# VectorE's paired instructions in the chunk scan of layer 2, joined into one each

## The chip, the core and the metric

The kernel runs on one core of one Trainium2 chip. The metric is device time in microseconds (us) of one launch; less is better. The engines of the core are named as the profile names them: PE (TensorE matmuls), DVE (VectorE), ACT (ScalarE), POOL (GpSimd) and SP (SyncE, which issues nearly all DMAs here).

## What is computed

Two blocks of a language model on one sequence of 1024 tokens with 1024 channels, in float32: layer 1 (a recurrent branch beside latent attention), layer 2 (a state-space layer), then a block with a short convolution, stick-breaking attention and an MLP. The change lies in layer 2, whose scan over chunks of 128 tokens is this, cut to what matters:

```python
xf = x * dt                                   # per head of 64 channels, 32 heads, 4 groups of 8 heads
cs = cumsum(dt * a_neg) within a chunk        # 8 chunks of 128 tokens
cb = einsum('bclgn,bcsgn->bcgls', cc, bc)     # per group, 128 x 128 per chunk
y_diag = einsum('bcghls,bcsghp->bclghp', cb * exp(cs_l - cs_s) (causal), xf)
states = einsum('bclgn,bclghp->bcghpn', bc, xf * exp(cs_end - cs))
prev   = the states carried over the chunks   # h * exp(cs_end) + state
y_off  = einsum('bclgn,bcghpn->bclghp', cc, prev) * exp(cs)
y = (y_diag + y_off + d_skip * x) * silu(z)
```

## The kernel before

Each float32 matmul is made as three products of rounded halves (`mm3`, lines 189, 193 and 194: high by high, low by high, high by low). A cast on ACT makes the high half and a subtraction in `lo` (line 260) the low one, on DVE in the scan and on POOL elsewhere. Weights come through `weights` in sets of three tiles `wr`, `wh`, `wl`: a DMA, a cast on ACT (line 180), a subtraction.

`phase_b` is layer 2. Its work comes in 8 units u (half a group, 4 heads, 256 channels), and each unit in 4 steps of two chunks, so 32 steps. A step has two parts:

- `stage1`: four transposes on PE into PSUM (line 891); `Xf`, the transposed x times dt and times w2, a [128 x 512] half each (line 898), then its halves `Xh` (ACT, line 902) and `Xl` (DVE, 260). `L`, [128 x 2 chunks x 4 heads x 128], is loaded from `csd` by one DMA (line 907), goes through eight Relus (911) and one Exp (913) on ACT, is multiplied by the group's `cbm` on DVE (916), and split into `Lh` (ACT, 918) and `Ll` (DVE). The tile `L` has one buffer, so the next load waits for this `Ll`. Then the states of both chunks (matmuls into a `t` bank, lines 934 to 940 for `hs`, `hh`, `hl`).
- `stage2`: the matmuls of y_off into a bank of PSUM, `et` loaded with exp(cs) by four DMAs (line 966), `zt` loaded from DRAM; then on DVE: `et` times that bank (971, or 973 and 974 in a unit's first step, whose first chunk has no state before it), the skip term (976, one instruction per tile of 128 channels), the sum with y_diag (988, four per step, 64 partitions each), and the product with z (991, one per tile). The result goes to DRAM (992); ACT squares it (997) and DVE adds the squares up (999 or 1002).

In `et` the 512 columns stand as (chunk, tile, token), in `zt` as (tile, chunk, token).

Between the steps stand projections: 48 matmuls of 512 columns each into one `g` tile (two banks), whose results go through ACT (lines 810, 812 or 873), and DVE. They are independent of the scan until their own unit needs them, and the loop at the end of `phase_b` deals them out by `PATTERN`; once all are made, `part` puts matmuls of the layer's output projection in their place. At the end of a group `prep_bc` makes the next group's `cbm` and the halves of B and C (lines 846 to 860).

The Python order is not the order on the chip: a scheduler places each engine's instructions when the program is built, by its own estimate of their durations, and each engine then works strictly in that order. PSUM has two `g` tiles, two `t` banks and one bank each of `u` and `w` here; the matmuls of y_off and y_diag take `u` and `w` in turn, so one of them can only start when DVE has read the bank before.

Of the kernel before, what the change touches and what calls it, by code (L numbers as in the profile page):

```python
# [12 lines left out]
A = mybir.AluOpType  # L13
# [5 lines left out]
HN = 512  # L19
# [30 lines left out]
class K:  # L50
# [38 lines left out]
    def v(self, name, i=0, n=1):  # L89
        o, _ = VEC[name]  # L90
        return self.vec[:, o + i:o + i + n]
# [657 lines left out]
    def phase_b(self):  # L749
# [14 lines left out]
        ps = first.pop(0)  # L764
# [115 lines left out]
        def stage1(u, cpair):  # L880

            g, hg = divmod(u, 2)
            h0 = 8 * g + 4 * hg
            c0 = 2 * cpair
            th, tl, ch, cl, cbm = bc[g]
            xt = xs[u]

            ps = self.t1()
            for c in range(2):
                for p in range(2):  # L890
                    nc.tensor.transpose(ps[:, c * 256 + p * 128:c * 256 + p * 128 + 128],
                                        xt[p][:, (c0 + c) * 128:(c0 + c) * 128 + 128], self.ident)
            Xf = P("Xf")
            for j, f in enumerate((dt_t, w2_t)):
                for c in range(2):
                    fb = f[:, (c0 + c) * 32 + h0:(c0 + c) * 32 + h0 + 4]
                    q = slice(c * 256, c * 256 + 256)
                    nc.vector.tensor_tensor(Xf[:, j * HN + c * 256:j * HN + c * 256 + 256].rearrange("p (h d) -> p h d", h=4),
                                            ps[:, q].rearrange("p (h d) -> p h d", h=4),
                                            fb[:, :, None].to_broadcast([128, 4, 64]), op=A.mult)  # L900
            Xh, Xl = R("Xh"), R("Xl")
            nc.scalar.copy(Xh, Xf)
            self.lo(nc.vector, Xl, Xf, Xh)

            L = self.tag("L", "L")
            Lv = L.rearrange("p (c h l) -> p c h l", c=2, h=4)
            nc.sync.dma_start(L.rearrange("p (c x) -> p c x", c=2),
                              csd[c0:c0 + 2, h0:h0 + 4, :].rearrange("c h l -> c (h l)").partition_broadcast(128))
            for c in range(2):
                for h in range(4):  # L910
                    nc.scalar.activation(Lv[:, c, h, :], Lv[:, c, h, :], AF.Relu, scale=-1.0,  # L911
                                         bias=cs_t[:, (c0 + c) * 32 + h0 + h:(c0 + c) * 32 + h0 + h + 1])
            nc.scalar.activation(L, L, AF.Exp, scale=-1.0)
            cv = cbm.rearrange("p (c l) -> p c l", c=8)
            for c in range(2):
                nc.vector.tensor_tensor(Lv[:, c], Lv[:, c], cv[:, c0 + c:c0 + c + 1, :].to_broadcast([128, 4, 128]), op=A.mult)
            Lh, Ll = R("Lh"), R("Ll")
            nc.scalar.copy(Lh, L)
            self.lo(nc.vector, Ll, L, Lh)

            prev = []
            pst = self.t1()
            for c in range(2):
                s = slice((c0 + c) * 128, (c0 + c) * 128 + 128)
                q = slice(HN + c * 256, HN + c * 256 + 256)
                prev.append(hst[u][1] if c0 + c else None)
                if c0 + c == 7:
                    break
                self.mm3(pst[:, c * 256:c * 256 + 256], (th[:, s], tl[:, s]), (Xh[:, q], Xl[:, q]), True, True)
                hn = self.ph.tile([128, 256], F32, tag="hs", bufs=2, name=self.nm("hs"))  # L930
                q = pst[:, c * 256:c * 256 + 256]
                if c0 + c:
                    dv = dec[:, h0:h0 + 4, c0 + c][:, :, None].to_broadcast([128, 4, 64])
                    nc.vector.tensor_tensor(hn.rearrange("p (h d) -> p h d", h=4), hst[u][0].rearrange("p (h d) -> p h d", h=4), dv, op=A.mult)
                    nc.vector.tensor_tensor(hn, hn, q, op=A.add)
                else:
                    nc.vector.tensor_copy(hn, q)
                hh = self.ph.tile([128, 256], F32R, tag="hh", bufs=4, name=self.nm("hh"))
                hl = self.ph.tile([128, 256], F32R, tag="hl", bufs=4, name=self.nm("hl"))
                nc.scalar.copy(hh, hn)  # L940
                self.lo(nc.vector, hl, hn, hh)
                hst[u] = hn, (hh, hl)
            stg[u, cpair] = Xh, Xl, Lh, Ll, prev

        def stage2(u, cpair):
            g, hg = divmod(u, 2)
            h0 = 8 * g + 4 * hg
            c0 = 2 * cpair
            th, tl, ch, cl, cbm = bc[g]
            xt = xs[u]  # L950
            Xh, Xl, Lh, Ll, prev = stg.pop((u, cpair))
            cols = slice(c0 * 128, c0 * 128 + 256)

            poff = self.u1()
            for c in range(2):
                if prev[c]:
                    hh, hl = prev[c]
                    s = slice((c0 + c) * 128, (c0 + c) * 128 + 128)
                    for p in range(2):
                        q = slice(p * 128, p * 128 + 128)  # L960
                        self.mm3(poff[:, c * 256 + p * 128:c * 256 + p * 128 + 128], (hh[:, q], hl[:, q]), (ch[:, s], cl[:, s]), True, True)
            et = self.E("et")
            ev = et.rearrange("p (c q l) -> p c q l", c=2, q=2)
            for j in range(2):
                for p in range(2):
                    nc.sync.dma_start(ev[64 * j:64 * j + 64, :, p, :], ecd[c0:c0 + 2, h0 + 2 * p + j, :].partition_broadcast(64))
            zt = self.E("zt")
            zv = zt.rearrange("p (q x) -> p q x", q=2)
            nc.sync.dma_start(zv, self.zd[u * 256:u * 256 + 256, cols].rearrange("(q p) x -> p q x", q=2))
            if c0:  # L970
                nc.vector.tensor_tensor(et, et, poff, op=A.mult)
            else:
                nc.vector.memset(et[:, 0:256], 0.0)
                nc.vector.tensor_tensor(et[:, 256:], et[:, 256:], poff[:, 256:], op=A.mult)
            for p in range(2):
                nc.vector.scalar_tensor_tensor(ev[:, :, p, :], xt[p][:, cols].rearrange("p (c l) -> p c l", c=2), v("d_skip", 4 * g + 2 * hg + p),
                                               ev[:, :, p, :], op0=A.mult, op1=A.add)

            for c in range(2):
                pd = self.u1()  # L980
                for p in range(2):
                    q = slice(c * 256 + p * 128, c * 256 + p * 128 + 128)
                    s = slice(c * HN + p * 256, c * HN + p * 256 + 256)
                    self.mm3(pd[:, p * 256:p * 256 + 256], (Xh[:, q], Xl[:, q]), (Lh[:, s], Ll[:, s]), True, True)
                pv = pd.rearrange("p (q j l) -> p q j l", q=2, j=2)
                for j in range(2):
                    r = slice(64 * j, 64 * j + 64)
                    nc.vector.tensor_tensor(ev[r, c], ev[r, c], pv[r, :, j, :], op=A.add)
            for p in range(2):
                z = zv[:, p, :].rearrange("p (c l) -> p c l", c=2)  # L990
                nc.vector.scalar_tensor_tensor(z, ev[:, :, p, :], 0.5, z, op0=A.mult, op1=A.mult)
            nc.sync.dma_start(self.yd[u * 256:u * 256 + 256, cols].rearrange("(q p) x -> p q x", q=2), zv)

            if g not in acc2:
                acc2[g] = P("acc2")
            sq = et
            nc.scalar.activation(sq, zt, AF.Square)
            if hg == 0:
                nc.vector.tensor_tensor(acc2[g][:, cols], sq[:, 0:256], sq[:, 256:], op=A.add)
            else:  # L1000
                for p in range(2):
                    nc.vector.tensor_tensor(acc2[g][:, cols], acc2[g][:, cols], sq[:, p * 256:p * 256 + 256], op=A.add)
                if cpair % 2:
                    n = cpair // 2
                    s = slice(n * HN, n * HN + HN)
                    ps = self.u1()
                    nc.tensor.matmul(ps, self.ones, acc2[g][:, s], start=True, stop=True)
                    self.rstd_from(acc2[g][:, s], ps, 1.0 / 512, 1e-6)
                    nc.sync.dma_start(self.rsd[g:g + 1, s], acc2[g][0:1, s])
# [919 lines left out]
```

## Time and profile before

| what | value |
|---|---|
| runs, us | 2761.08, 2748.82, 2758.09; median 2758.09 |
| profiled execution, us | 2749.49 |
| its span, first to last instruction, us | 2747.7 |
| busy in the span, us | PE 2590.2, DVE 1933.3, ACT 1438.8, POOL 655.1 |
| mean granted TensorE clock | 0.975 of full |
| the scan of layer 2 in the trace | from about 570 to 1280 us |
| attention of the second block in the trace | from about 1680 to 1990 us |

A busy share is an average over stages with different limits; idle time of an engine that nobody waits for costs nothing. A wait is put down to the instruction whose end released it.

### The profile page before, as it was taken

Reading aid. Unit: us, or ns where it says so; the run is one execution under the profiler, and the core shown is the slowest. Engines: PE = TensorE matmul, PEld = TensorE weight load, DVE = VectorE, ACT = ScalarE, POOL = GpSimd, SP = SyncE. Lnnn points to the kernel's source line nnn. Section 1 sums busy time; section 2 is a strip of 40 time slices with the busy share of each in tenths; the row PEclk is TensorE's granted clock in tenths of the full one; section 3 lists DMA queues with packets and bytes.
Section 4 is the critical chain, followed back from the end, with each engine's and each line's share of the span. In section 5 each row is a group of like instructions: output and inputs, shape, how many; then the busy total and the mean of one; then the engine's idle time right before and its main releaser. Section 6 shows DMA issues by size and latency. Waiting matters only on the chain. (4 is left out here: it accounts for less than half of the span.)

```text
span 2747.7 us, 34501 instructions
## 1 busy us (share of the span) xinstructions
PE 2590.2 (94%) x12000; PEld 2077.2 (76%) x12000; DVE 1933.3 (70%) x2754; ACT 1438.8 (52%) x2447; POOL 655.1 (24%) x467
## 2 busy tenths in 40 slices
PE   8999999999989899789989999998899999999997
PEld 6777887787877788677767776766688888887786
DVE  5683766769978698785575215889696666777577
ACT  5553754656656555543463224665665455443465
POOL 2642754400000000004455324566300000000024
PEclk9999999999999999889999999999999999999999
DMA  4444533443434344366443334543454446977324
GB/s 128 159 159 142 139 93 108 151 133 115 139 103 134 113 125 138 94 217 221 141 133 92 125 130 123 159 118 98 161 207 148 148 152 222 336 245 238 120 72 152
DMA packets 214419, 407.14 MB, mean 148 GB/s; under 512 B 22636, under 2 KB 61548, under 8 KB 214244
## 3 DMA queue, kind: packets, MB, share of 16 engines
q1 hardware_dynamic: 214244, 404.93, 45.9%
q8 instruction: 94, 1.54, 0.2%
q14 instruction: 81, 0.66, 0.1%
HBM read 297.35 MB, written 107.50 MB: 147 GB/s over the span
## 5 line engine op out<-in xcount | busy, mean ns | idle before, releaser
L260 POOL TENSOR_TENSOR wl<-wr,wh 128x512 fp32r<-128x512 f32 (+2 forms) x262 | 371.5, 1422 | 1158.4 <-ACT wh L180 1105.3
L189 PE MATMUL g<-XH,wh 128*128 128x512 f32 x1296 | 525.3, 406 | 23.8 <-ACT xc L812 10.3
L193 PE MATMUL g<-XL,wh 128*128 128x512 f32 x1296 | 523.7, 404 | 4.6 <-DVE XL L746 2.4
L194 PE MATMUL g<-XH,wl 128*128 128x512 f32 x1296 | 521.1, 402 | 4.7 <-POOL wl L260 4.7
L180 ACT CAST wh<-wr 128x512 fp32r<-128x512 f32 (+2 forms) x367 | 221.0, 604 | 395.5 <-PE g L193 164.8
L189 PEld LDWEIGHTS g<-XH,wh 128*128 128x128 f32 x1296 | 248.3, 192 | 85.1 <-ACT xc L812 11.3
L193 PEld LDWEIGHTS g<-XL,wh 128*128 128x128 f32 x1296 | 248.2, 192 | 65.4 <-DVE XL L260 4.4
L194 PEld LDWEIGHTS g<-XH,wl 128*128 128x128 f32 x1296 | 248.1, 191 | 64.8 <-POOL wl L260 6.3
L260 DVE TENSOR_TENSOR wl<-wr,wh 128x512 fp32r<-128x512 f32 (+1 forms) x198 | 133.0, 683 | 75.4 <-ACT wh L1531 45.0
L260 POOL TENSOR_TENSOR yl<-yl,yh 128x1024 fp32r<-128x1024 f32 x4 | 9.6, 2400 | 715.0 <-ACT yh L1075 712.3
L193 PE MATMUL m<-XL,XH 128*128 128x512 f32 x368 | 144.8, 393 | 5.5 <-DVE XL L260 5.5
L189 PE MATMUL m<-XH,XH 128*128 128x512 f32 x368 | 143.7, 392 | 0.0
L194 PE MATMUL m<-XH,XL 128*128 128x512 f32 x368 | 143.6, 392 | 0.0
L911 ACT ACTIVATE L<-L,tm 128x128 f32<-128x128 f32 x256 | 78.8, 389 | 122.4 <-DMA L<-csd 116.4
L194 PE MATMUL t<-XH,wl 128*128 128x512 f32 (+1 forms) x328 | 129.4, 395 | 1.3 <-POOL wl L260 1.2
L189 PE MATMUL t<-XH,wh 128*128 128x512 f32 (+1 forms) x328 | 128.2, 391 | 1.0 <-ACT wh L180 1.0
L193 PE MATMUL t<-XL,wh 128*128 128x512 f32 (+1 forms) x328 | 128.5, 392 | 0.0
L1615 ACT CAST XH<-a 128x1024 fp32r<-128x1024 f32 x46 | 48.2, 1049 | 134.6 <-PE m L193 109.3
L1283 DVE TENSOR_TENSOR_SCAN kp<-kp,zero 128x640 f32<-128x640 f32 (+5 forms) x64 | 107.0, 1693 | 5.5 <-ACT kp L1279 3.8
L1284 POOL TENSOR_TENSOR sg<-sg,kp 128x639 f32<-128x639 f32 (+5 forms) x64 | 91.3, 1436 | 75.5 <-DVE kp L1283 71.9
L577 ACT CAST XL<-t 128x512 fp32r<-128x512 f32 (+2 forms) x192 | 78.4, 426 | 46.1 <-DVE XL L260 21.2
L260 DVE TENSOR_TENSOR XL<-t,XL 128x512 fp32r<-128x512 f32 (+2 forms) x192 | 87.5, 472 | 14.8 <-ACT XL L577 14.0
(584 smaller groups left out, 6519.4 us busy)
## 6 DMA issues: line engine op xcount, KB each, us to landing
a<-w_down SPq DMA_DIRECT2D x64, 512.0 KB, 4.8
b<-hd SPq DMA_DIRECT2D x48, 512.0 KB, 5.7
wr<-wb_in SPq DMA_DIRECT2D x90, 256.0 KB, 2.7
wr<-wc_in SPq DMA_DIRECT2D x72, 256.0 KB, 2.8
L<-csd SPq DMA_DIRECT2D x32, 512.0 KB, 6.4
wr<-w_up SPq DMA_DIRECT2D x28, 512.0 KB, 4.9
wr<-wb_out SPq DMA_DIRECT2D x48, 256.0 KB, 4.7
hd<-t SPq DMA_DIRECT2D x48, 256.0 KB, 2.3
```

What stands on the lines that cost most here:

```text
L180: nc.scalar.copy(hi[:, :n], raw[:, :n])
L189: first = nc.tensor.matmul(ps, w[0], a[0], start=start, stop=False, skip_group_check=more)
L193: nc.tensor.matmul(ps, w[0], a[1], start=False, stop=False, skip_group_check=more)
L194: nc.tensor.matmul(ps, w[1], a[0], start=False, stop=stop, skip_group_check=more)
L260: eng.tensor_tensor(out, src, hi.bitcast(F32), op=A.subtract)
L577: nc.scalar.copy(th[:, y], ps[:, x])
L911: nc.scalar.activation(Lv[:, c, h, :], Lv[:, c, h, :], AF.Relu, scale=-1.0, bias=cs_t[:, (c0 + c) * 32 + h0 + h:(c0 + c) * 32 + h0 + h + 1])
L1283: nc.vector.tensor_tensor_scan(rv, rv, zero.to_broadcast([128, W]), 1.0, op0=A.mult, op1=A.add)
L1284: nc.gpsimd.tensor_tensor(sg[:, :W - 1], sg[:, :W - 1], kp[:, 1:W], op=A.mult)
L1615: nc.scalar.copy(hi, x)
```

## The change

Where two VectorE instructions of a step treat its two chunks, or its two tiles of 128 channels, one instruction now treats both: `Xf` takes two instructions per step and not four, the product with `cbm` one and not two, the product with z one and not two. For that `et` takes the column order of `zt`, (tile, chunk, token). The instructions on `et` that were already one (971, 973, 974, 988) keep their number and size and read or write the new order; 976 stays two per step, now on 256 columns in a row. No matmul, no ACT instruction and no DMA is added or removed.

```diff
@@ stage1
-                for c in range(2):
-                    fb = f[:, (c0 + c) * 32 + h0:(c0 + c) * 32 + h0 + 4]
-                    q = slice(c * 256, c * 256 + 256)
-                    nc.vector.tensor_tensor(Xf[:, j * HN + c * 256:j * HN + c * 256 + 256].rearrange("p (h d) -> p h d", h=4),
-                                            ps[:, q].rearrange("p (h d) -> p h d", h=4),
-                                            fb[:, :, None].to_broadcast([128, 4, 64]), op=A.mult)
+                fb = f.rearrange("p (c h) -> p c h", h=32)[:, c0:c0 + 2, h0:h0 + 4]
+                nc.vector.tensor_tensor(Xf[:, j * HN:j * HN + HN].rearrange("p (c h d) -> p c h d", c=2, h=4),
+                                        ps.rearrange("p (c h d) -> p c h d", c=2, h=4),
+                                        fb[:, :, :, None].to_broadcast([128, 2, 4, 64]), op=A.mult)
...
-            for c in range(2):
-                nc.vector.tensor_tensor(Lv[:, c], Lv[:, c], cv[:, c0 + c:c0 + c + 1, :].to_broadcast([128, 4, 128]), op=A.mult)
+            nc.vector.tensor_tensor(Lv, Lv, cv[:, c0:c0 + 2, None, :].to_broadcast([128, 2, 4, 128]), op=A.mult)
@@ stage2
-            ev = et.rearrange("p (c q l) -> p c q l", c=2, q=2)
+            ev = et.rearrange("p (q c l) -> p c q l", c=2, q=2)
...
-                nc.vector.tensor_tensor(et, et, poff, op=A.mult)
+                nc.vector.tensor_tensor(ev, ev, poff.rearrange("p (c q l) -> p c q l", c=2, q=2), op=A.mult)
...
-                nc.vector.memset(et[:, 0:256], 0.0)
-                nc.vector.tensor_tensor(et[:, 256:], et[:, 256:], poff[:, 256:], op=A.mult)
+                nc.vector.memset(ev[:, 0], 0.0)
+                nc.vector.tensor_tensor(ev[:, 1], ev[:, 1], poff[:, 256:].rearrange("p (q l) -> p q l", q=2), op=A.mult)
             for p in range(2):
-                nc.vector.scalar_tensor_tensor(ev[:, :, p, :], xt[p][:, cols].rearrange("p (c l) -> p c l", c=2), v("d_skip", 4 * g + 2 * hg + p),
-                                               ev[:, :, p, :], op0=A.mult, op1=A.add)
+                q = slice(p * 256, p * 256 + 256)
+                nc.vector.scalar_tensor_tensor(et[:, q], xt[p][:, cols], v("d_skip", 4 * g + 2 * hg + p), et[:, q], op0=A.mult, op1=A.add)
...
-            for p in range(2):
-                z = zv[:, p, :].rearrange("p (c l) -> p c l", c=2)
-                nc.vector.scalar_tensor_tensor(z, ev[:, :, p, :], 0.5, z, op0=A.mult, op1=A.mult)
+            nc.vector.scalar_tensor_tensor(zt, et, 0.5, zt, op0=A.mult, op1=A.mult)
```

DVE has 128 instructions fewer. The scheduler, which sees other durations, also places the rest anew, from the first steps of the scan to the end of the second block's attention, on all engines; before and after that stretch the orders are the same. Three places of it follow. The change is five lines shorter, so its line numbers from 896 on differ: its 909, 911, 915 and 937 are 911, 913, 918 and 940 of before, and its 1268, 1269 and 1271 are 1273, 1274 and 1276.

**First place: PE, the start of the second group** (u = 2), just ahead of its first y_diag matmuls. `t_6855` (in the change `t_6817`) holds states, `t_6988` (`t_6949`) is a target of transposes, `g_7098` (`g_7055`) the projection that fills the time. Before:

```order
L891 MATMUL t_6988<-ident_r,xc_6530 128x128
L891 MATMUL t_6988<-ident_r,xc_6367 128x128
L891 MATMUL t_6988<-ident_r,xc_6530 128x128
L194 MATMUL g_7098<-XH_68,wl_7094 128x512
L189 MATMUL g_7098<-XH_69,wh_7093 128x512
L193 MATMUL g_7098<-XL_77,wh_7093 128x512
```

The change:

```order
L194 MATMUL g_7055<-XH_71,wl_7051 128x512
L891 MATMUL t_6949<-ident_r,xc_6340 128x128
L891 MATMUL t_6949<-ident_r,xc_6499 128x128
L891 MATMUL t_6949<-ident_r,xc_6340 128x128
L891 MATMUL t_6949<-ident_r,xc_6499 128x128
L189 MATMUL t_6817<-Xh_6797,bth_6560 128x256
L193 MATMUL t_6817<-Xl_6798,bth_6560 128x256
L194 MATMUL t_6817<-Xh_6797,btl_6561 128x256
L189 MATMUL w_6865<-Lh_6635,Xh_6619 128x256
```

Before, 18 projection matmuls stand between these transposes and the next states matmul; in the change none do, they stand ahead of `prep_bc`. From the last matmul of `prep_bc` to the last y_diag matmul of u's first two steps there are 175 matmuls before, 108 of them of projections, and 147 in the change, 80 of them of projections.

**Second place: ACT, the same seam.** `wh` are casts of weights, `L_7002` (in the change `L_6961`) is the L of the unit's third step, `hh` casts of states. Before:

```order
L918 CAST Lh_6851<-L_6838 128x1024
L180 CAST wh_7251<-wr_7250 128x512
L940 CAST hh_6862<-hs_6859 128x256
L911 ACTIVATE L_7002<-L_7002,tm 128x128 x8
L180 CAST wh_7413<-wr_7412 128x512
L913 ACTIVATE L_7002<-L_7002 128x1024
```

The change:

```order
L915 CAST Lh_6813<-L_6801 128x1024
L937 CAST hh_6655<-hs_6652 128x256
L180 CAST wh_7362<-wr_7361 128x512
L937 CAST hh_6824<-hs_6821 128x256
L909 ACTIVATE L_6961<-L_6961,tm 128x128 x8
L937 CAST hh_6834<-hs_6831 128x256
L911 ACTIVATE L_6961<-L_6961 128x1024
```

The cast of the next projection's first weights (`wh_7413`, in the change `wh_7362`) stood behind the Relus of L_7002 and now stands ahead of them.

**Third place: PE, the start of the second block's attention.** `s` are score matmuls, `t` transposes of weights of attention, `f` matmuls of the output projection. Before:

```order
L1273 MATMUL s_14356<-XL_75,XL_73 128x128
L1274 MATMUL s_14356<-kl_14282,XL_73 128x128
L1276 MATMUL s_14356<-mask,ident_r 128x128
L574 MATMUL t_14397<-ident_r,sg_14313 128x128
L189 MATMUL f_14458<-hh_14291,wh_14461 128x512
L1273 MATMUL s_14364<-XL_75,XL_73 128x256
```

The change:

```order
L189 MATMUL f_14330<-hh_14163,wh_14333 128x512
L1268 MATMUL s_14228<-XL_75,XL_73 128x128
L1269 MATMUL s_14228<-kl_14154,XL_73 128x128
L1271 MATMUL s_14228<-mask,ident_r 128x128
L1268 MATMUL s_14236<-XL_75,XL_73 128x256
L1269 MATMUL s_14236<-kl_14154,XL_73 128x256
```

The first `f` matmul has moved ahead of a block of scores, and the first transpose behind two of them; from here on the rows of this stage stand in another order, with the same rows in sum.

## Rows read from the trace of the kernel before

**Rows 1.** The page, part 1: busy time, share of the span, instructions.

```profile
PE 2590.2 (94%) x12000; PEld 2077.2 (76%) x12000; DVE 1933.3 (70%) x2754; ACT 1438.8 (52%) x2447; POOL 655.1 (24%) x467
```

**Rows 2.** Stretches: scan, attention; us, busy PE, PEld, DVE, ACT, POOL, PEclk, DMA share, GB/s.

```profile
570.00:1280.00 710.00, 656.70 (x3244) 544.54 (x3245) 586.95 (x1008) 389.71 (x667) 12.12 (x6) 0.95 0.45 138
...
1680.00:1990.00 310.00, 282.07 (x1346) 203.96 (x1347) 255.17 (x315) 192.86 (x391) 165.47 (x114) 0.95 0.45 133
```

**Rows 3.** Stretches: two of six around the scan's PE gaps, and all six's sum.

```profile
770.00:800.00 30.00, 21.31 (x99) 16.96 (x98) 20.35 (x42) 17.74 (x34) 0.00 (x0) 0.80 0.29 79
...
1105.00:1131.00 26.00, 15.10 (x64) 13.37 (x63) 17.87 (x41) 15.12 (x31) 0.00 (x0) 0.70 0.30 79
...
sum 149.00, PE 100.47 PEld 82.61 DVE 119.91 ACT 86.90 POOL 0.00; mean PE 16.74 PEld 13.77 DVE 19.98 ACT 14.48 POOL 0.00
```

**Rows 4.** Waits of PE, 570 to 1300: who waited for whom, us, times, longest.

```profile
PE t L189 <- ACT Xh L902: 16.0, 7, 5.3
PE g L189 <- ACT xc L812: 10.3, 4, 3.7
```

**Rows 5.** Waits of ACT and DVE, 570 to 1300.

```profile
ACT L L911 <- DMA L<-csd: 116.4, 28, 9.2
...
DVE et L973 <- DMA et<-ecd: 9.6, 4, 3.2
```

**Rows 6.** Groups on DVE, 570 to 1300, shapes apart: busy us, mean ns of one | idle before.

```profile
L898 DVE TENSOR_TENSOR Xf<-t,tm 128x256 f32<-128x256 f32 x128 | 45.5, 415 | 4.3 <-PE t L891 4.0
L916 DVE TENSOR_TENSOR L<-L,cbm 128x512 f32<-128x512 f32 x64 | 41.6, 684 | 2.5 <-ACT L L913 2.1
L260 DVE TENSOR_TENSOR Xl<-Xf,Xh 128x1024 fp32r<-128x1024 f32 x32 | 39.1, 1223 | 30.3 <-ACT Xh L902 30.1
...
L976 DVE SCALAR_TENSOR_TENSOR et<-xc,vec,et 128x256 f32<-128x256 f32 x64 | 27.9, 477 | 0.1
...
L991 DVE SCALAR_TENSOR_TENSOR zt<-et,zt 128x256 f32<-128x256 f32 x64 | 24.3, 419 | 0.2
...
L874 DVE SCALAR_TENSOR_TENSOR z<-z,g 128x1024 f32<-128x1024 f32 x16 | 19.5, 1217 | 0.9 <-ACT z L873 0.7
...
L1074 DVE SCALAR_TENSOR_TENSOR yl<-yl,vec,rs 128x1024 f32<-128x1024 f32 x12 | 15.2, 1279 | 2.2 <-DMA yl<-yd 2.1
...
L860 DVE SCALAR_TENSOR_TENSOR cbm<-mask,t 128x512 f32<-128x512 f32 x8 | 5.5, 684 | 0.5 <-PE t L194 0.4
```

**Rows 7.** Timeline of DVE at the second group's start: start us, us to the last's end.

```profile
789.49 0.69 DVE L260 TENSOR_TENSOR wl<-wr,wh 128x512 fp32r<-128x512 f32 x1 [4.71 <-ACT wh L180]
...
790.97 1.29 DVE L916 TENSOR_TENSOR L<-L,cbm 128x512 f32<-128x512 f32 x2
...
793.24 0.76 DVE L991 SCALAR_TENSOR_TENSOR zt<-et,zt 128x256 f32<-128x256 f32 x2
...
795.03 1.41 DVE L898 TENSOR_TENSOR Xf<-t,tm 128x256 f32<-128x256 f32 x4
```

**Rows 8.** Timeline of ACT, same place.

```profile
786.50 2.44 ACT L911 ACTIVATE L<-L,tm 128x128 f32<-128x128 f32 x8 [5.48 <-DMA L<-csd]
...
795.45 1.21 ACT L812 ACTIVATE xc<-g,hw 128x1024 f32<-128x1024 f32 x1
```

**Rows 9.** Timeline of PE, ahead of that place and at it.

```profile
743.22 0.39 PE L189 MATMUL g<-XH,wh 128*128 128x512 f32 x1
...
746.95 0.39 PE L193 MATMUL g<-XL,wh 128*128 128x512 f32 x1
...
791.09 0.55 PE L189 MATMUL w<-Lh,Xh 128*128 128x256 f32 x1 [5.55 <-DVE et L988]
...
796.72 0.79 PE L189 MATMUL g<-XH,wh 128*128 128x512 f32 x1 [1.70 <-ACT xc L812]
```

**Rows 10.** Waits of PE in attention, 1680 to 1990.

```profile
PE u L585 <- DVE XL L260: 6.7, 5, 1.9
PE f L189 <- DVE tp L690: 6.3, 3, 3.9
```

## The prediction

> **What bounds the kernel now.** I read the page's busy times first, then the stretches, then PE's waits in the scan, and last the timelines around the longest of them. The reader should see that PE is busy 94% of the span and DVE 70% [rows 1], so DVE work costs time only where PE waits for it. In the scan of layer 2, where the change lies, PE is busy 656.7 of 710 us: 53.3 us are open, and the mean clock granted to it is 0.95 [rows 2]. Nearly all of this lies in six short places, where units and groups meet and the projection matmuls that otherwise fill PE's queue run short. Together these are 149 us long and PE works in 100.5 of them, so 48.5 us are open there; in two of them the granted clock is 0.80 and 0.70 [rows 3], that is, a part of the stretch at 1.2 GHz and the rest at 2.4, after PE had stood. The waits themselves are named by what comes last: the cast Xh, and the convolution's ACT pass `xc` [rows 4].
>
> What is behind both is one chain. L has one buffer. ACT waited 116.4 us in all, 28 times, for the load of L, up to 9.2 us at once [rows 5], and everything behind the eight Relus in ACT's queue waits with it. At the second group's start one sees it whole: the Relus of L start at 786.5 after 5.48 us of waiting [rows 8]; a weight cast stood behind them, DVE's subtraction `wl` waited 4.71 us for that cast [rows 7], the sums of y (line 988) stood behind `wl`, and PE waited 5.55 us for the bank that these sums free; then it waited 1.70 us for `xc` [rows 9], whose pass (795.45) stood behind the Relus too [rows 8].
>
> **The change part by part.** What is removed: 64 instructions of Xf, 32 of L times cbm, 32 of y times z. Alone, an instruction of 256 columns takes 415 to 419 ns, one of 512 takes 684, one of 1024 takes 1217 to 1223 [rows 6]. Back to back the ends overlap, and this is how they mostly stand: two of L take 1.29 us together, two of z 0.76, four of Xf 1.41 [rows 7]. Joined they should take 1.22, 0.68 and 1.29 (the last as the row with two of 512). The gain per step is 0.07 + 0.08 + 0.12 = 0.27 us, 8.6 us of DVE over 32 steps. Where none stood back to back, by single durations, it would be 64 x (830 - 684) + 32 x (1368 - 1223) + 32 x (838 - 684) ns = 9.3 + 4.6 + 4.9 = 18.8 us. I take 8.6, since the pairs' own rows show it.
>
> Here a rule speaks for more. The rows show that single instructions carry a fixed part (512 more columns cost 1223 - 684 = 539 ns, so of the 684 some 145 are not columns), but that a pair back to back pays only some 70 ns of it twice. The Trainium skill ("VectorE: DVE Perf Modes", section on the fixed extra latency per instruction) gives (N + 151) / 0.96 ns for a float32 tensor_tensor, so by it each joined pair saves 157 ns and all 128 save an estimated 20.1 us. It agrees with the single rows and not with the pairs'.
>
> How much of the 8.6 us lies on the path? Where PE works through projections, nothing: they cover it, and if that cover went, the whole would count. At the six places the chain runs through about two steps each; 12 x 0.27 us is 3.2 us. I take -3, with 0 and -8.6 as bounds.
>
> What is re-laid costs nothing, as far as rows tell. Line 976 takes 477 ns on split columns and line 991 419 on split columns of the same number, so it is not the split; 1279 against 1217 at 1024 columns shows the same 62 ns for an operand with a scalar per partition [rows 6]. If the split did cost them, the gain is 64 x 60 ns = 3.8 us of DVE, covered like the rest. Instructions 971 and 974 now write split columns; the row of line 860, which has a repeated operand, takes the same 684 as a plain one [rows 6], and I take 0; even 60 ns on each of 32 would be 1.9 us of DVE. The et loads move the same pieces of 128 floats to another column; DVE's waits for them in the unit's first step sum to 9.6 us [rows 5], which bounds a change there at that much either way, and I take 0.
>
> What is moved: the schedule. At the second group's start 28 projection matmuls go from behind `prep_bc` to ahead of it. They start 0.233 us apart (16 steps from 743.22 to 746.95 [rows 9]), so 6.5 us of cover is gone from the chain that begins with `prep_bc`. Against that, the weight cast is now ahead of the Relus, so DVE no longer stands the 4.71 us. That frees the bank, but does not start PE's next projection: what is late next is `xc`, still behind the Relus in ACT's queue. The chain itself is shorter in the new order by what no longer stands in it: z's product of 1.2 us [rows 6], a `wl` of 0.7 [rows 7] and the cast ahead of it, which I put at the same, some 2.6 us. The place would cost 6.5 - 2.6 = 3.9 us; bounds +6.5 (all the cover) and -4.7 (the freed wait was all that counted). I take +3. At the other groups' starts the order of PE is the same or a few matmuls off.
>
> In attention the rows stand in another order, without a shared direction that I could read; PE's open time there is 310 - 282.1 = 27.9 us [rows 2], and I take 0.
>
> **The sum**: -3 + 3 + 0 = 0. Against the profiled execution that is 2749.5 us. That execution is 8.6 us under the median of the runs; the four executions known have a mean of 2754.4, and I put the forecast there: **2754 us**. A measurement of this kernel can tell about 0.5% (14 us) from no change, so faster means below 2744.3 and slower above 2771.9, against the median of 2758.1.
>
> **The rivals.**
>
> *All of the gain reaches the end.* The joined instructions save their single durations, 18.8 us, and each of it lies in the chain of some step: 2754.4 - 18.8 = 2736. For it speaks that every joined instruction has a cast on ACT behind it (Xh, Lh, the square of z), and Xh is PE's first wait [rows 4]. Against it: the pairs' rows, and that PE is covered outside the six places. By the formula of the Trainium skill cited above ("VectorE: DVE Perf Modes") it would be an estimated 2734.
>
> *The seams close.* The new order, casts ahead of the Relus in more places, takes a third off the 48.5 us at the six places: -16, or 2738. For it: the wait of 5.55 us [rows 9] shows how one misplaced cast stops three engines. Against: most seams keep their order, and the load of L stays.
>
> *Attention gets worse.* The slower side: one mechanism, the new order of attention, in which `f` matmuls that filled PE's waits for DVE's halves `XL` and sums `tp` (6.7 and 6.3 us, up to 3.9 at once [rows 10]) come sooner and are missing later. If PE stands as long again there, the time is 2754.4 + 27.9 = 2782; it decides from 17.5 us, 63% of that. For it: this stage is not touched by the change, so nothing is gained in it to pay for the new order. Against it: the same 12 `f` matmuls follow each other in much the same places from its middle on.
>
> *The joined form does not do what it says.* With two chunks, four heads and a repeated operand it runs at half rate. Then Xf alone adds 64 x 0.68 = 44 us to DVE, and the 12 steps in the seams 12 x 1.4 = 16 us to the time: 2770. Against it: line 898 and line 860 already repeat an operand, at the plain duration [rows 6].
>
> **How the numbers follow.** The forecast has 0.53 (its own range, by the bounds above and 6 us of spread between runs, is 2741 to 2768; 0.03 of it beyond each limit). All the gain: 0.05, and the seams: 0.19, both faster but for 0.01. Attention: 0.17, slower but for 0.01. The half rate: 0.06, half of it slower. Faster is 0.03 + 0.23 = 0.26, slower 0.03 + 0.16 + 0.03 = 0.22, the same 0.52. For 8 in 10 the range reaches towards both rivals and leaves out their far ends: 2734 to 2780.
>
> **What would show it.** In the profile of the changed kernel: Xf as 64 instructions near 684 ns, L times cbm as 32 near 1220, z as 32 near 684; 976 still at 477; DVE's busy time in the scan about 8 us down. PE's open time in the scan should stay within 10 us of 53; at the second group's start PE should stand longer than the 30 - 21.3 = 8.7 us before [rows 3], but not for line 988 after `wl`. Open time in attention should stay near 28. The prediction is wrong if PE's open time in either stage moves by over 14 us, or if the joined instructions take more than 10% over those durations.

## The result, and the profile after

The changed kernel takes 2771.8 us (median of 9 runs, 2764.7 to 2789.2) against 2757.2 (9 runs, 2748.8 to 2762.4): a ratio of 1.0061, 95% interval 1.0044 to 1.0077. It is slower by some 17 us by that ratio, 14.6 between the medians; the forecast was 2754, no change. The profiled execution takes 2769.8 us, its span 2768.0. First the page, part 1, of the kernel after, to be held against [rows 1]:

```profile
PE 2615.1 (94%) x12000; PEld 2097.0 (76%) x12000; DVE 1925.4 (70%) x2626; ACT 1439.7 (52%) x2447; POOL 666.2 (24%) x467
```

DVE is 7.9 us less busy. PE is 24.9 us more busy, with the same 12000 matmuls; its open time went down, from 2747.7 - 2590.2 = 157.5 us to 152.9. So PE does not stand longer: its matmuls take longer. How much is in part chance: the profiled execution of the kernel before was granted a mean clock of 0.975, and the 88 executions of that kernel beside the runs below were granted 0.961 to 0.971. But the medians point the same way: 0.966 to 0.968 for the kernel before, 0.961 in the nine executions of the change. By them the lower clock costs an estimated 17 us of PE's time at full speed, (1 - 0.961) x 2771.8 less (1 - 0.967) x 2757.2, or less where PE stood at that clock. The stretches of scan and attention (us, busy PE, PEld, DVE, ACT, POOL, PEclk, DMA share, GB/s), as [rows 2]:

```profile
570.00:1285.00 715.00, 663.96 (x3268) 550.52 (x3266) 578.20 (x878) 390.65 (x667) 9.92 (x4) 0.94 0.44 136
...
1690.00:2005.00 315.00, 291.63 (x1352) 210.39 (x1351) 251.79 (x312) 190.60 (x386) 175.16 (x115) 0.92 0.45 133
```

In the scan 51 us are open (53.3 before), in attention 23.4 (27.9 before), and the mean granted clock is lower in both; the stretches hold 24 and 6 matmuls more than those of [rows 2]. The joined instructions are what they were meant to be. Groups on DVE, 570 to 1305, as [rows 6]:

```profile
L896 DVE TENSOR_TENSOR Xf<-t,tm 128x512 f32<-128x512 f32 x64 | 41.4, 686 | 4.7 <-PE t L891 4.5
...
L913 DVE TENSOR_TENSOR L<-L,cbm 128x1024 f32<-128x1024 f32 x32 | 39.0, 1220 | 0.4 <-ACT L L911 0.2
L974 DVE SCALAR_TENSOR_TENSOR et<-xc,vec,et 128x256 f32<-128x256 f32 x64 | 27.9, 477 | 0.1
...
L986 DVE SCALAR_TENSOR_TENSOR zt<-et,zt 128x512 f32<-128x512 f32 x32 | 24.2, 755 | 0.2
```

Only the product with z has an odd mean, 755 ns: one of the 32 took 2.87 us, of which more below.

To find where the time went I matched the k-th instruction of each group in both traces and followed by how much it starts later. Four places stand out: the second group's start (700 to 940 us), the fourth group's start (1100 to 1260), the hand-over from the scan's last step to what follows (1260 to 1320), and the start of attention (1660 to 1740). The first and the third say most.

### The profile page after: what moved, and what is told of

It reads as the page before. It is cut to its first block, busy times and chain, and to the rows that moved or that the text cites. A ratio compares the mean times of both kernels' runs of the same rounds, so it can differ in the third digit from the quotient of the medians.

```text
span 2768.0 us, 34375 instructions
## 1 busy us (share of the span) xinstructions
PE 2615.1 (94%) x12000; PEld 2097.0 (76%) x12000; DVE 1925.4 (70%) x2626; ACT 1439.7 (52%) x2447; POOL 666.2 (24%) x467
## 4 chain that ended last, share of the span: by engine, by line
PE 38%; DVE 5%; ACT 3%; DMA 2%; issue 2%; POOL 0%; SPq 0%; DVEq 0%; ACTq 0%; POOLq 0%
PE m L189 6%; PE m L193 6%; PE m L194 6%; PE g L194 2%; PE g L193 2%; PE g L189 2%; PE t L189 2%; PE t L194 2%; PE t L193 2%; DMA a<-w_down 1%; DVE XL L260 1%; PE s L1269 1%; PE t L574 1%; PE f L189 1%; PE f L193 1%
## 5 line engine op out<-in xcount | busy, mean ns | idle before, releaser
L260 POOL TENSOR_TENSOR wl<-wr,wh 128x512 fp32r<-128x512 f32 (+2 forms) x262 | 378.3, 1447 | 1167.2 <-ACT wh L180 1115.5
```

What stands on the lines that cost most here:

```text
L260: eng.tensor_tensor(out, src, hi.bitcast(F32), op=A.subtract)
```

## The experiments

The change does two things at once: it joins instructions, and it lets the scheduler place everything else anew. To part them, a list of places was added that ties each engine's instructions to each other in a given order, by edges that carry no wait:

```diff
+def pin_order(nc, tc):
...
+    for e, (n, first, text) in PLACES.items():
+        ins = by[e]
...
+        for a, b in zip(at, at[1:]):
+            tc.add_manual_dep(ins[b], ins[a].name, mybir.DependencyInfo(mybir.DependencyClass.NoSync, mybir.DependencyReason.DATA), reason="order")
...
 def tile_kernel(ctx, tc, d, out):
     K(ctx, tc, d).run(out)
+    pin_order(tc.nc, tc)
```

"Old order" is that of the kernel before on PE, DVE, ACT, POOL and SP, "new order" that of the change. All but the second run below have the change's instructions and differ in the list alone; the second is the kernel before with the list of the change. The kernel before with its own order tied was not run, so what the list itself costs is not shown.

**1. Joined, old order.**

> The change's instructions, with every engine's queue in the order of the kernel before (a joined instruction stands where the second of its pair stood). Order theory (the joined instructions cost nothing, the 14.6 us come from where the scheduler put the rest): back at the time before, ratio to before 0.997 to 1.001, and the hand-over after the scan's last step, which in the change stretched by 9.6 us, as short as before. Form theory (the joined instructions themselves hold up the chains; the last product with z took 2.87 us in the change's profile): stays slower, ratio 1.003 or more.

Measured: 2753.9 us, ratio 0.9981 (0.9969 to 0.9993). The joined instructions are a small gain, 0.19% or 5.2 us (1.9 to 8.5), once nothing else moves.

**2. Not joined, new order.**

> The instructions and layout of the kernel before, in the order that the change has on every engine (the two of a pair follow each other where the joined one stands). Order theory: as slow as the change, ratio to before 1.004 to 1.008, VectorE 8 us busier. Form theory: as fast as before, 0.998 to 1.002.

Measured: 2783.5 us, 1.0079 (1.0055 to 1.0104). The order alone makes the loss; in this order, too, the joined form comes out 0.0018 better than the pairs (1.0061 against 1.0079), which is less than their intervals. The form theory has fallen.

**3 and 4. New order in one stage, old in the other** (the list changes sides at 1300 us, in a stretch where both orders agree).

> The change with its own order up to 1300 us and the order of before in the second block's attention. If the hand-over at the scan's end carries most of it: ratio 1.003 to 1.005. If the order of attention does (6 us of the profiled difference arose there): 1.000 to 1.002.

> The mirror of the run with the scan new and attention old: the order of before up to 1300 us, the change's own in attention. If the hand-over carries most of it: ratio 0.998 to 1.001. If attention does: 1.002 to 1.005. The two mirrored runs' differences should add up to that of the change, 0.5% to 0.6%.

Measured: scan new, attention old 1.0045 (1.0027 to 1.0063); scan old, attention new 0.9991 (0.9974 to 1.0008). Against run 1 the scan's new order costs 0.0064, some 17.6 us. The new order of attention costs 0.0010, which the intervals don't tell from nothing. The traces of the third run show losses at the second group's start and at the hand-over, so the next four took the scan apart.

**5 to 8. Old order but for a part of the scan.** A is all up to 935 us (the second group's start), C 1095 to 1274 us (the fourth group's start), D the rows after it, at the scan's last step. In A it is the first and second place shown ahead of the prediction that differ most. C and D in rows of the order, where they differ from the old (D also has PE's sum of squares three matmuls earlier and ACT's Ln of that sum ahead of one cast XH):

```
C, SP +L1034 DMA t<-x1d x4
      +L1066 DMA rs<-rsd
       L1004 DMA rsd<-acc
       L1038 DMA x1p<-t
       L179 DMA wr<-wb_out
      -L1034 DMA t<-x1d x4
      -L1066 DMA rs<-rsd
       L1068 DMA yl<-yd
...
D, DVE
     +L1069 SCALAR_TENSOR_TENSOR yl<-yl,vec,rs
      L985 TENSOR_TENSOR et<-et,w x2
     -L1069 SCALAR_TENSOR_TENSOR yl<-yl,vec,rs
     +L260 TENSOR_TENSOR wl<-wr,wh
      L986 SCALAR_TENSOR_TENSOR zt<-et,zt
     -L260 TENSOR_TENSOR wl<-wr,wh
```

> The joined instructions in the old order, with the change's order up to 935 us alone (the scan's first half, the second group's start in it). Against the joined instructions wholly in the old order (ratio to before 0.9981). In the profiles so far this stretch takes some 6 us more in the new order than in the old, nearly all of it from the second group's start on: 0.9981 + 0.0022 = 1.0003, and the PE-open time around that start grows. If instead the hand-over after the scan's last step carries the whole loss: 0.998.

> Old order, the change's order from 1095 to 1274 us alone (the fourth group's start; the loads of yl stand later in SyncE's queue). By the profiles so far some 2 to 3 us: 0.999. If the late yl alone, without its place ahead of the last sums, held up the hand-over: 1.001 or more.

> Old order but for the twelve or so rows of the hand-over after the scan's last step: on VectorE the product yl (which waits for its load) stands ahead of the last two sums of y, and a subtraction wl ahead of the product with z; on TensorE the sum of squares stands three matmuls earlier. If the place of yl alone costs what the hand-over lost (6 to 9 us): 1.000 to 1.0015. If it costs only when yl also lands late, as the change's order of SyncE makes it: 0.998.

> Old order up to 1095 us, the change's from there to the scan's end, old in attention: both the late loads of yl and its place ahead of the last sums. If the two together make the wait: 0.9981 + 0.0009 + 0.0024 = 1.0015 or more, while each alone costs under 0.001. With the run with the new order up to 935 us it should add up to the 1.0045 of the whole scan in the new order.

| new order in | ratio | interval | against run 1 |
|---|---|---|---|
| A | 1.0010 | 0.9997 to 1.0023 | +0.0029 |
| C | 1.0024 | 1.0009 to 1.0039 | +0.0043 |
| D | 1.0008 | 0.9993 to 1.0023 | +0.0027 |
| C and D | 1.0022 | 1.0008 to 1.0036 | +0.0041 |

A difference of two such ratios has an interval of its own, some 0.0018 or 5 us either way. A and (C and D) add up to 0.0070, near the 0.0064 of the whole scan. C and D add up to 0.0070 apart and to 0.0041 together, a difference at the edge of what the intervals allow. The profiles say it more clearly: the work of the hand-over, 253 to 260 matmuls, takes 60 us in run 1, 67 with C, 66 with D and 69 with both. So either alone is enough for most of the loss there, against what I expected of C alone (2 to 3 us). The profiles show both places.

*The second group's start.* Stretches of run 1 (old order), the first with 987 matmuls:

```profile
690.00:900.00 210.00, 196.07 (x987) 162.67 (x986) 177.88 (x280) 122.39 (x213) 0.00 (x0) 0.96 0.45 131
...
755.00:770.00 15.00, 15.00 (x73) 12.15 (x72) 8.21 (x11) 7.85 (x9) 0.00 (x0) 1.00 0.40 124
...
870.00:885.00 15.00, 12.48 (x62) 10.09 (x61) 13.82 (x23) 7.54 (x16) 0.00 (x0) 0.98 0.54 147
```

The same of run 5 (A new), where 984 matmuls take 217 us:

```profile
690.00:907.00 217.00, 202.31 (x984) 167.86 (x983) 178.68 (x281) 123.97 (x216) 0.00 (x0) 0.93 0.43 126
...
755.00:770.00 15.00, 12.58 (x53) 10.22 (x52) 11.31 (x19) 2.04 (x3) 0.00 (x0) 0.77 0.41 139
...
870.00:885.00 15.00, 12.79 (x50) 10.44 (x51) 12.82 (x22) 9.48 (x16) 0.00 (x0) 0.77 0.41 98
```

Seven us more, of which 6.2 are busy time (196.1 to 202.3) and 0.8 open (13.9 to 14.7): the granted clock falls in more stretches, to a mean of 0.93. (In the last pair run 1's clock falls a little later: it is 0.93 from 885 to 905, where run 5 has 1.00.) One profile does not fix the size: for 984 matmuls there the kernel before takes 210 us, the change's own profile 212, run 5 217 and run 3 218. PE's waits in run 5, by its timeline (start, us, what, and in brackets the idle time before and what ended it):

```profile
757.80 0.33 PE L193 MATMUL t<-cl,bh 128*128 128x128 f32 x1 [2.42 <-DVE cl L260]
...
790.56 0.38 PE L189 MATMUL t<-Xh,bth 128*128 128x256 f32 x1 [1.61 <-DVE hs L932]
...
794.14 0.45 PE L189 MATMUL u<-ch,hh 128*128 128x128 f32 x1 [2.26 <-DVE et L985]
```

The old order has one long wait there, 5.43 us for `et`, and none at `cl`. From run 1:

```profile
791.26 0.55 PE L189 MATMUL w<-Lh,Xh 128*128 128x256 f32 x1 [5.43 <-DVE et L985]
```

The new order has several shorter ones, the one for `cl` some 30 us ahead of the others: the open time is the same, but the clock falls more often. What comes first is `cl`, the half of C that `prep_bc` needs. DVE's timeline before:

```profile
744.41 1.22 DVE L260 TENSOR_TENSOR cl<-bc,ch 128x1024 fp32r<-128x1024 f32 x1
...
748.49 0.27 DVE L973 MEMSET et<- 128x256 f32 x1 [1.14 <-DMA et<-ecd]
```

and in run 5:

```profile
755.67 0.27 DVE L970 MEMSET et<- 128x256 f32 x1 [5.75 <-DMA et<-ecd]
755.86 0.75 DVE L974 SCALAR_TENSOR_TENSOR et<-xc,vec,et 128x256 f32<-128x256 f32 x2
756.52 1.22 DVE L260 TENSOR_TENSOR cl<-bc,ch 128x1024 fp32r<-128x1024 f32 x1
```

The first instruction of unit 2's `et` waits for its load, 5.75 us, and `cl` now stands behind it; ACT's `ch` was done at 749.5 (748.48 + 1.05). In the change's own profile this wait is the longest of eight, as the waits of DVE show (570 to 1300; 9.6, 4 and 3.2 in [rows 5], and 11.0, 4 and 3.5 in run 1):

```profile
DVE et L970 <- DMA et<-ecd: 18.8, 8, 5.9
```

*The hand-over.* The same work in the kernel before (257 matmuls) and in the change (255):

```profile
1260.00:1320.00 60.00, 57.66 (x257) 45.95 (x256) 30.24 (x35) 20.78 (x31) 33.48 (x23) 1.00 0.58 182
```

```profile
1264.00:1333.00 69.00, 61.09 (x255) 47.87 (x254) 33.13 (x34) 20.89 (x31) 34.32 (x23) 0.93 0.51 161
```

Nine us for nearly the same matmuls: 5.6 open, 3.4 at the lower clock. DVE's timeline before:

```profile
1270.96 0.85 DVE L988 TENSOR_TENSOR et<-et,w 64x256 f32<-64x256 f32 x2 [1.14 <-PE w L194]
1271.84 1.29 DVE L1074 SCALAR_TENSOR_TENSOR yl<-yl,vec,rs 128x1024 f32<-128x1024 f32 x1
1273.04 0.76 DVE L991 SCALAR_TENSOR_TENSOR zt<-et,zt 128x256 f32<-128x256 f32 x2
...
1274.78 2.70 DVE L1002 TENSOR_TENSOR acc<-acc,et 128x256 f32<-128x256 f32 x2 [0.38 <-ACT et L997]
...
1274.35 2.39 POOL L260 TENSOR_TENSOR yl<-yl,yh 128x1024 fp32r<-128x1024 f32 x1 [2.66 <-issue]
...
1297.66 0.50 PE L194 MATMUL t<-yh,wl 128*128 128x512 f32 x1 [2.34 <-POOL wl L260]
```

and after (in both, POOL's row and PE's waits stand behind DVE's):

```profile
1274.72 0.85 DVE L985 TENSOR_TENSOR et<-et,u 64x256 f32<-64x256 f32 x2
1279.17 1.28 DVE L1069 SCALAR_TENSOR_TENSOR yl<-yl,vec,rs 128x1024 f32<-128x1024 f32 x1 [3.60 <-DMA yl<-yd]
1280.48 0.85 DVE L985 TENSOR_TENSOR et<-et,w 64x256 f32<-64x256 f32 x2
1281.36 0.69 DVE L260 TENSOR_TENSOR wl<-wr,wh 128x512 fp32r<-128x512 f32 x1
1281.97 2.87 DVE L986 SCALAR_TENSOR_TENSOR zt<-et,zt 128x512 f32<-128x512 f32 x1
1285.54 0.88 DVE L997 TENSOR_TENSOR acc<-acc,et 128x256 f32<-128x256 f32 x2 [0.69 <-ACT et L992]
...
1281.67 2.62 POOL L260 TENSOR_TENSOR yl<-yl,yh 128x1024 fp32r<-128x1024 f32 x1 [4.80 <-ACT yh L1070]
...
1286.57 2.04 PE L1002 MATMUL u<-acc,ones_r 128*128 128x512 f32 x2 [2.97 <-DVE acc L997]
...
1306.80 0.80 PE L189 MATMUL t<-yh,wh 128*128 128x512 f32 x1 [3.66 <-ACT wh L180]
```

The product `yl` is for the next stage and waits for a load. In the new order it stands ahead of the last sums of y, which were ready, and holds them and the product with z for 3.6 us. The z product then meets POOL's subtraction and takes 2.87 us. That is no part of the loss, odd as it looks: before, the sums of the squares (`acc`) met POOL's subtraction and took 2.70 us and not 0.88, and from the start of the z product to the end of these sums it is 4.4 us both times (1273.04 to 1277.48, 1281.97 to 1286.42). Behind the z product hangs a chain to the next stage: squares, PE's sum of them, Ln and Exp on ACT, the store and load of the result, the next `yl`, the casts XH, and behind these in ACT's queue the weight casts `wh`, for which PE stands 3.66 us. With D alone the z product takes 2.90 us too, and PE waits 4.77 us for `wh`; with C alone no z product is odd (the sums of squares are, at 3.69 us), but PE waits 5.29 us: SP issues the fourth load of `yl` 9.2 us after the third there, and 7.7 us in run 1. So the chain seems to have no slack. With D or C new PE stands 3.7 to 5.8 us for `wh` in every profile. The old order is not safe either: in run 4, with the old rows, one such wait took 4.39 us, and the hand-over 66 us in that execution.

**9 and 10. The second group's start, PE alone.** Old order but PE's rows there (some 210 matmuls) new; and A new but these rows of PE old. The core of it, in rows of the order (`g` are projections, `w<-ch,hh` the y_off of the first group's last step, `t` the products of `prep_bc`):

```
     -MATMUL w<-ch,hh, w<-cl,hh, w<-ch,hl x12
      MATMUL g x24
     -MATMUL t<-ch,bh x2
      MATMUL g x3
     +MATMUL g x3, w<-ch,hh, w<-cl,hh, w<-ch,hl x12, g x23
      MATMUL w<-Lh,Xh, w<-Ll,Xh, w<-Lh,Xl x6
     +MATMUL t<-ch,bh x2, g x2
      MATMUL t<-cl,bh
...
     -MATMUL g x28
```

> Old order on every engine, but TensorE's queue around the second group's start (some 210 matmuls) as in the change: projection matmuls ahead of the products of prep_bc and not behind them. Cover theory (the loss there comes from TensorE, which meets cb's product before VectorE has the half cl, and later stands again with a lower granted clock): ratio to before 1.000 to 1.001 against 0.9981 for the old order, a wait for cl of 2 us or more in the profile. Rival (the other engines' new order there makes the loss): 0.998.

> The mirror: the change's order up to 935 us on all engines, but TensorE's old one around the second group's start. Cover theory: 0.998, or down to 0.9965 if the weight cast that now stands ahead of the Relus saves the 5.4 us for which TensorE stood there. Rival (the other engines): 1.001 as with the whole stretch new.

Measured: 1.0006 (0.9993 to 1.0019) and 1.0077 (1.0057 to 1.0097). Run 9: moving PE's projections alone costs 0.0025 against run 1, some 7 us with an interval of 5 either way, as the cover theory has it, but not by the wait that I named. (In its one profile the place costs less: 981 matmuls take 212 us, where run 1's 987 take 210.) PE's last use of the old group's `ch` moved behind projections as well, and ACT, which overwrites it, waits 5.70 us for it:

```profile
755.72 1.05 ACT L851 CAST ch<-bc 128x1024 fp32r<-128x1024 f32 x1 [5.70 <-PE w L193]
```

PE finds `cl` ready, since it comes later itself, and stands further on:

```profile
792.27 0.58 PE L189 MATMUL t<-Xh,bth 128*128 128x256 f32 x1 [2.89 <-DVE hs L932]
...
802.59 0.55 PE L189 MATMUL w<-Lh,Xh 128*128 128x256 f32 x1 [4.16 <-DVE et L985]
```

Run 10 misses by far and says nothing on the question: the old rows of PE among the others' new ones make waits of their own, 6.78 us for `et` and 5.36 for `cl`.

**11 and 12. Towards a better order.** Joined, old order, and one row of ACT moved at the second group's start; then also the rstd at the hand-over:

```
ACT  +L180 CAST wh_7362<-wr_7361
      L909 ACTIVATE L_6961<-L_6961,tm x8
     -L180 CAST wh_7362<-wr_7361
...
ACT   L1088 CAST XH_64<-yl
     +L291 ACTIVATE acc<-u,eps, L294 ACTIVATE acc<-acc, with their table loads
      L1088 CAST XH_65<-yl, XH_66<-yl
     -L291 ACTIVATE acc<-u,eps, L294 ACTIVATE acc<-acc, with their table loads
```

> Joined instructions, old order, and one row of ScalarE's queue moved: at the second group's start the weight cast wh stands ahead of the eight Relus of L and not behind them. As the prediction has it, the 5.4 us for which TensorE waits for line 985 go, and what is late next is xc, still behind the Relus: most of the gain is given back, 0.997 to 0.998. If the freed wait were all that counted: 0.9964.

> The run with one cast ahead, and at the hand-over after the scan's last step the Ln and Exp of the last group's sum of squares (with their table loads) moved ahead of two casts XH that wait for loads. Chain theory of the hand-over (last product with z, squares, rstd, its store and load, yl, XH, and the weight casts behind XH): the chain ends some 2.5 us earlier, TensorE's wait of 2.3 us for wl goes: a further 0.0008 off, and no execution with a longer wait there. Rival (the hand-over is held by the loads of yl alone): no change against the run with one cast ahead.

Measured: 0.9975 (0.9961 to 0.9990) and 0.9965 (0.9949 to 0.9982). Run 12, with a median of 2745.7 us against 2755.8 beside it, is faster than the kernel before and than the change. Each of the two steps beyond run 1 is smaller than its interval. In run 11 (its profiled execution is its slowest of 12, at 2764.1 us) the wait of 5.43 us for line 985 is down to 0.75, and the next two have it:

```profile
790.70 0.36 PE L189 MATMUL w<-Lh,Xh 128*128 128x256 f32 x1 [0.75 <-DVE et L985]
...
796.29 0.58 PE L189 MATMUL u<-Lh,Xh 128*128 128x256 f32 x1 [4.64 <-DVE et L968]
799.56 0.79 PE L189 MATMUL g<-XH,wh 128*128 128x512 f32 x1 [1.63 <-ACT xc L812]
```

At the hand-over of run 12 PE's wait for `wl` stays at 2.05 us (2.35 in run 1), so the mechanism that I expected is not shown, and nothing decides against its rival.

## Why the prediction was wrong

In short: the price of the joined instructions was right, that of the new order was not. The forecast looked for the order's cost at six known waits of PE and put it at nothing elsewhere; the largest loss, some 9 us, lay at the hand-over, outside them. And it priced stops by their open time alone, with no term for the clock.

- **The joined instructions: right.** 686, 1220 and, in run 1, 686 ns (755 in the change, with the one of 2.87 us in it) against the 684, 1220 and 684 named; line 974 at 477. Their three groups take 102.3 us in run 1 (41.3, 39.0 and 22.0) against 111.4 in [rows 6]: 9.1 us less, 8.6 predicted. The Trainium skill's formula ("VectorE: DVE Perf Modes", section on the fixed extra latency per instruction) would have made it an estimated 20.1; the measurement decides for the pairs' rows.
- **What of it lies on the path: near.** -3 us, bounds 0 and -8.6; run 1 gives -5.2, within the bounds.
- **The re-layout at nothing: no sign against it**, since run 1 has the new layout and is faster. **The loads of `et`, taken at 0 with 9.6 us as the bound either way: this step failed.** The layout did next to nothing to them (11.0 us in run 1), but the order did: DVE's waits for them rose by 9.2 us to 18.8, and I did not ask what would stand behind the waiting row.
- **The second group's start, +3 us: too small by the times, with the size left open.** Runs 5 and 9 cost 8.0 and 6.9 us against run 1, as much as the upper bound (+6.5, all the cover gone) or more; the interval of 5 us either way just reaches down to +3, and the change's own profile shows some 2 there. The 2.6 us that I had taken off for a shorter chain do not show in the times. That the freed wait for line 985 would be followed by the next one was right: in run 11 it is 4.64 us for `et` of line 968 first, and `xc` after it. I priced the place by PE's cover and by open time, and expected PE to stand longer. The open time stayed nearly the same (13.9 us in run 1 and 14.7 in run 5; 8.7 from 735 to 803 in the kernel before and 9.7 from 735 to 810 in the change); in run 5 the matmuls took 6.2 us longer, at the lower clock that followed the new stops. The profile of before had shown that clock, 0.80 and 0.70 at two seams [rows 3], and the sum had no term for it: this step failed.
- **"At the other groups' starts the order of PE is the same or a few matmuls off": this step failed.** It looked at PE's rows alone, and at group starts alone. At the scan's end, where before PE has one wait of 2.34 us and so none of my six places lay, a row of DVE that waits for a load went ahead of two that don't; the place lost 9 us. C and D together cost 11.3 us against run 1.
- **Attention at 0: right as far as the runs tell.** The rival that attention gets worse fell: against run 1 its new order costs 0.0010 in run 4, within the intervals, and not the 17.5 us from which it was to decide. The 5 us more of the one profile of the change (315 against 310, with 6 matmuls more) mislead.
- **The other rivals** fell: not all gain arrived, the seams did not close by themselves, and no joined form ran at half rate.
- **The test that I set failed as a test.** Open time in the scan stayed within 10 us of 53 (it is 51) and in attention within 5 of 28, and still the kernel lost 17 us.

So the sum should have been -5 (joined) +7 (second group) +11 (fourth group's start and hand-over) and about 3 for attention, unresolved: +16, against the 14.6 between the medians. Each term is uncertain by several us, so that they meet is in part luck. Open remain the share of the rows of D, which were not moved one at a time, which rows of C make the late load, what the fourth group's start costs without the hand-over (C holds both), and the mirror of run 9.

## What to carry to other kernels

Where a scheduler places instructions by estimated durations, an edit that shortens some is two changes; pin the old order to see what the edit itself is worth, and cost the new order at every place where a row that waits for a load has come ahead of a row on a chain, on each engine, not only at the known waits. Price a stop of TensorE by the time that the same matmuls take around it, clock included, not by its open time. Before blaming a stage for a few us in one profile, look at the same stage in several executions.

## What the runs showed of the hardware that I had not expected

**Two engines at one instruction.** The z product that starts 0.30 us after POOL's subtraction took 2.87 us (2.88 to 2.90 in runs 3, 7 and 8) where it takes 0.69 alone, and ended 0.55 us after POOL's (1281.67 + 2.62). The Trainium skill ("SBUF — State Buffer", section "SBUF: two separate sides") says that VectorE and GpSimd share a port pair as an exclusive lock, held for a whole instruction by the one that starts first, when VectorE's has two SBUF inputs and GpSimd's reads SBUF. The trace agrees with that: POOL's started first, and the z product reads `et` and `zt`, both in SBUF. It is not new with the change: before, the sums of squares met it.

**The clock after a stop.** At the start of attention the same rows in the same order went different ways. In run 1 PE's granted clock stays at half, the level of 1.2 GHz, for 37 us, in which PE has no time open at all. Three stretches of them:

```profile
1695.00:1705.00 10.00, 10.00 (x32) 7.12 (x30) 10.00 (x16) 4.58 (x12) 8.28 (x8) 0.50 0.34 94
1705.00:1715.00 10.00, 10.00 (x32) 7.27 (x32) 7.03 (x11) 4.73 (x11) 5.65 (x6) 0.50 0.22 66
1715.00:1725.00 10.00, 10.00 (x35) 7.37 (x34) 4.79 (x10) 4.40 (x12) 2.35 (x4) 0.50 0.46 144
```

In run 5 it falls later and is back at full within 7 us, though PE stands 1.8 us and 0.9 us there:

```profile
1705.00:1715.00 10.00, 8.21 (x28) 5.71 (x26) 9.99 (x14) 4.58 (x12) 8.74 (x9) 0.66 0.52 109
1715.00:1725.00 10.00, 9.08 (x52) 6.81 (x51) 9.65 (x14) 6.59 (x17) 6.18 (x7) 1.00 0.54 157
```

The stay is 7 us long in the kernel before too, some 20 us in six of the 14 profiles, and 37 us or more in four (runs 1, 3 and 11; 51 in run 2). Against the kernel before, these four lose 9 to 14 us by the shift of equal instructions from 1660 to 1750 us, more than any single edit here gained. What decides how long it stays was not tried.
